# Hi and lo of the MLP activations in one matmul of 512 columns

## The chip, the cores and the metric

The kernel runs on one NeuronCore of a Trainium2 chip. The metric is the device time of one execution in microseconds (us). A run gives a median over several executions; one more execution is profiled, and all rows of a trace come from that one.

## The reference

A four-layer encoder on 256 tokens of width 1024, all in float32. Each layer is a mixer (a state-space layer in layers 0 and 3, dilated attention in 1, differential attention in 2) and an MLP, both with a residual and a norm in front. The change is in the four MLPs:

```python
def rmsnorm(x, g):
    xf = x.astype(jnp.float32)
    y = xf * lax.rsqrt(jnp.mean(xf * xf, axis=-1, keepdims=True) + RMS_EPS)
    return (y * g.astype(jnp.float32)).astype(x.dtype)
...
def sqrelu_mlp(h, w1, w2):
    return jnp.square(jax.nn.relu(h @ w1)) @ w2
...
        x = x + h
        x = x + sqrelu_mlp(rmsnorm(x, norm_mlp_g[i]), mlp_w1[i], mlp_w2[i])
```

`w1` is 1024x4096 and `w2` 4096x1024, so an MLP reads 32 MB of weights for 256 tokens.

## The kernel before

Activations lie transposed: features on the 128 partitions, the 256 tokens (`T`) along the free axis. A product is made of tiles: a 128x128 tile of weights stands in TensorE (a weight load, LDWEIGHTS), and the 256 tokens stream through it (a matmul of 256 columns). Float32 accuracy comes from splitting: every weight and every activation is written as hi + lo in the type fp32r, and a tile product is three matmuls into the same 256 columns of a PSUM bank, hi x hi, hi x lo and lo x hi. That is `mm3`, lines 150, 151 and 152, each matmul with its own weight load. This text calls the work on one weight tile a *trio*.

Weights come in chunks of 128x1024 (512 KB). `_dma` asks SP's queue for a chunk into `raw` (5 buffers), `_conv` makes `whi` on ScalarE (ACT, line 117) and `wlo` on VectorE (DVE, line 119), 5 buffers each; `plan_chunk` fixes the order of the chunks beforehand, `take` and `done` step through it. A chunk feeds 8 trios.

The MLP, `mlp`, runs over 8 strips `s` of 512 hidden features. `up(s)` makes a strip, 4 chunks and 32 trios, into two banks (`r0`/`r1` or `r2`/`r3`), two 256-column results side by side in a bank. `evac(s)` turns it into the input of the second product: on DVE `v` (relu, times the norm's factor, line 358), on ACT the square (line 360) and the hi part `hh` (line 362), on DVE the lo part `hl` (line 363), each on 128x512. `down(s)` multiplies the strip by its rows of `w2`, 4 chunks and 32 trios, and adds to 8 output tiles that lie two to a bank in `a0` to `a3` through the whole MLP. The order is up 0, up 1, down 0, up 2, down 1, and so on; the last strip goes tile by tile (`proj_tail`), and after each tile `finish` adds it to the residual `xT` (line 1179) and makes the next part's split inputs `spl` (lines 234, 235) and squares.

For strip 0, and in the first MLP for strip 4, the first half of the hidden features lies in a tile of its own, `h0`/`l0` (`same` in the code; `h` and `l` in the rows). In the first MLP, after strip 2, `bias_vectors` and `lambdas` use the banks `r2` and `r3` for three small products of the later attention layers (lines 732, 733, 748).

Each engine works through its own queue in order; a scheduler lays out the queues when the kernel is built. The trace's 490 `whi` and 490 `wlo` instructions are all chunks of all parts. Matmuls in plain float32 (line 148, tile `nf`) stand in the two state-space layers.

Of the kernel before, what the change touches and what calls it, by code (L numbers as in the profile page):

```python
# [24 lines left out]
NSPL = 16  # L25
# [26 lines left out]
class Prog:  # L52
# [92 lines left out]
    def mm3(self, out, wh, wl, xh, xl, start, stop):  # L145
# [6 lines left out]
        mm(out, lhsT=wl, rhs=xh, start=False, stop=stop, skip_group_check=True)  # L152

# [65 lines left out]
    def split_tile(self):  # L219
        return self.sp.tile([P, 2, T], F32R, tag="spl", name="spl", bufs=NSPL)  # L220

    def norm_begin(self):
        self.sqs = []
        self.uh, self.ul = [], []

    def norm_split(self, j, g, perm, x):
# [3 lines left out]
        if j % 2 == 0:  # L230
            h, lo = self.split_tile(), self.split_tile()
            self.uh += [h[:, 0, :], h[:, 1, :]]
            self.ul += [lo[:, 0, :], lo[:, 1, :]]
# [60 lines left out]
    def normalised_tiles(self, keep):  # L294
        self.nhl = [self.lp.tile([P, KD, T], F32R, name=n) for n in ("nh", "nl")]
        self.nf = self.lp.tile([P, KD, T], F32, name="nf") if keep else None

    def normalised(self, g_mix):

        nc = self.nc  # L300
        nh, nl = self.nhl
# [5 lines left out]
        return nh, nl  # L307


    def plan_mlp(self, l):  # L310
        w1, w2 = self.a["mlp_w1"], self.a["mlp_w2"]
        def up(s):
            for j in range(4):
                self.plan_chunk(("up", l, s, j), w1[l, j * 256:(j + 1) * 256, s * 512:(s + 1) * 512].rearrange("(k p) f -> p k f", p=P))
        def down(s):
            for j in range(4):
                self.plan_chunk(("dn", l, s, j), w2[l, (4 * s + j) * P:(4 * s + j + 1) * P, :].rearrange("(k p) f -> p k f", p=P))
        up(0)
        for s in range(1, 8):
            up(s)  # L320
            down(s - 1)
        for key, ap in self.tail_chunks(("dn", l), w2[l], 28, 4):
            self.plan_chunk(key, ap)

    def mlp(self, l, finish):
        nc = self.nc
        hs = {}
        acc = [self.bank(f"a{i}") for i in range(4)]

        def up(s):  # L330
            b = [self.bank(f"r{2 * (s % 2) + i}") for i in range(2)]
            for j in range(4):
                wh, wl = self.take(("up", l, s, j))
                for kk in range(2):
                    k = 2 * j + kk
                    for n in range(4):
                        c = slice(kk * 512 + n * P, kk * 512 + (n + 1) * P)
                        self.mm3(b[n // 2][:, (n % 2) * T:(n % 2 + 1) * T], wh[:, c], wl[:, c],
                                 self.uh[k], self.ul[k], k == 0 and n % 2 == 0, k == 7)
# [3 lines left out]

        self.lp.tile([P, 80], F32, name="gap0")
        same = [self.lp.tile([P, 2, T], F32R, name=n) for n in ("h0", "l0")]
        self.lp.tile([P, 48], F32, name="gap1")
        resets = (0,) if self.rep else (0, 4)

        def evac(s, b):
            hh = self.lp.tile([P, 4, T], F32R, tag="hh", name="hh", bufs=2)  # L350
            hl = self.lp.tile([P, 4, T], F32R, tag="hl", name="hl", bufs=2)
            hs[s] = [(hh[:, j, :], hl[:, j, :]) for j in range(4)]
            if s in resets:
                hs[s][:2] = [(same[0][:, j, :], same[1][:, j, :]) for j in range(2)]
            for i in range(2):
                v = self.lp.tile([P, 2, T], F32, tag="v", name="v", bufs=3)
                sq = self.lp.tile([P, 2, T], F32, tag="vsq", name="vsq", bufs=2)
                nc.vector.scalar_tensor_tensor(out=v, in0=b[i].rearrange("p (n t) -> p n t", n=2), scalar=0.0,
                                               in1=self.rbc.unsqueeze(1).to_broadcast([P, 2, T]), op0=ALU.max, op1=ALU.mult)
                nc.scalar.activation(out=sq, in_=v, func=AF.Square)  # L360
                h, lo = (hh[:, 2 * i:2 * i + 2, :], hl[:, 2 * i:2 * i + 2, :]) if i or s not in resets else same
# [3 lines left out]
        def down(s):  # L365
            h = hs.pop(s)
            if s < 7:
                for j in range(4):
                    wh, wl = self.take(("dn", l, s, j))
                    for n in range(8):  # L370
                        c = slice(n * P, (n + 1) * P)
# [794 lines left out]
    def prepare_part(self, i):  # L1166
# [8 lines left out]
        def finish(n, acc, perm=False):  # L1175
# [8 lines left out]
            if nxt == "final":  # L1184
                self.final_tile(n)
# [114 lines left out]
```

## Time and profile before

| what | us |
|---|---|
| runs of the kernel before: median, lowest, highest of 3 | 1605.35, 1604.55, 1608.08 |
| profiled execution: its time | 1607.9 |
| profiled execution: span from the first to the last instruction | 1606.1 |
| TensorE busy in the span | 1566.8 (98%) |
| VectorE busy, ScalarE busy | 1203.5, 960.3 |

The profiled execution's time is 1.8 us over its span and 2.55 us over the median. Busy time of TensorE overlaps itself, since matmuls are pipelined: a row gives each 256-column matmul some 280 ns, while one starts every 113 to 120 ns. What one costs is read from start to start.

### The profile page before, as it was taken

The numbers are of one execution on the slowest core, as the hardware profiler recorded it, in microseconds if no ns is written. First come the engines' busy times: TensorE is split into PE (matmuls) and PEld (weight loads), VectorE is DVE, ScalarE is ACT, GpSimd is POOL, SyncE is SP. The second block draws the span as 40 slices with busy tenths as digits, with TensorE's granted clock in tenths as the row PEclk, the third lists the DMA queues.
The fourth block names the chain that finished last, engine by engine and source line by source line (L and its number), as shares of the span: only waits on it lengthen the run. The fifth ranks groups of instructions, "written<-read, shape, count | busy, mean of one in ns | idle before, by whom it ended". The sixth has DMA issues, their size and how long they took to land.

```text
span 1606.1 us, 32218 instructions
## 1 busy us (share of the span) xinstructions
PE 1566.8 (98%) x12942; PEld 1519.4 (95%) x12942; DVE 1203.5 (75%) x1970; ACT 960.3 (60%) x1620; POOL 134.1 (8%) x120
## 2 busy tenths in 40 slices
PE   9999999999999999999999999999998999999998
PEld 8889899999999999999999999999988988899997
DVE  6999998455697777766556898655588999995554
ACT  6586865444667666655445777444455767664444
POOL 0012121000300000010000101000011122310001
PEclk9999999999999999999999999999999999999999
DMA  7677755676566555546666764666655767656661
GB/s 230 195 223 236 213 188 181 204 223 191 159 200 178 151 170 162 171 148 190 191 196 187 198 193 122 205 192 193 189 163 155 217 210 216 210 173 195 192 193 64
DMA packets 230293, 299.83 MB, mean 187 GB/s; under 512 B 16496, under 2 KB 166256, under 8 KB 230144
## 3 DMA queue, kind: packets, MB, share of 16 engines
q1 hardware_dynamic: 209552, 262.51, 53.4%
q10 hardware_dynamic: 20592, 35.27, 8.0%
q8 instruction: 101, 1.65, 0.4%
q14 instruction: 48, 0.39, 0.1%
HBM read 296.41 MB, written 3.62 MB: 187 GB/s over the span
## 4 chain that ended last, share of the span: by engine, by line
PE 73%; DVE 14%; DMA 5%; ACT 4%; issue 3%; POOL 1%; ACTq 0%; SPq 0%; DVEq 0%; POOLq 0%
PE r L151 12%; PE r L150 12%; PE r L152 12%; PE a L150 8%; PE a L152 8%; PE a L151 8%; DVE wlo L119 3%; DMA raw<-in_ssd_in_w_dram 2%; DMA bc<-scr 2%; PE r L148 2%; DVE cvx L488 1%; PE a L857 1%; PE a L858 1%; PE a L856 1%; DVE bc L582 1%
## 5 line engine op out<-in xcount | busy, mean ns | idle before, releaser
L119 DVE TENSOR_TENSOR wlo<-raw,whi 128x1024 fp32r<-128x1024 f32 (+1 forms) x490 | 592.8, 1217 | 291.4 <-ACT whi L117 287.9
L117 ACT CAST whi<-raw 128x1024 fp32r<-128x1024 f32 (+1 forms) x490 | 503.4, 1034 | 436.3 <-PE r L151 223.6
L151 PE MATMUL r<-spl,whi 128*128 128x256 f32 x1696 | 472.9, 279 | 4.7 <-DVE spl L235 4.7
L150 PE MATMUL r<-spl,whi 128*128 128x256 f32 x1696 | 475.1, 280 | 0.1
L152 PE MATMUL r<-spl,wlo 128*128 128x256 f32 x1696 | 471.4, 278 | 0.4 <-DVE wlo L119 0.4
L151 PEld LDWEIGHTS r<-spl,whi 128*128 128x128 f32 x1696 | 318.4, 188 | 6.5 <-DVE spl L235 6.1
L152 PEld LDWEIGHTS r<-spl,wlo 128*128 128x128 f32 x1696 | 318.6, 188 | 0.7 <-DVE wlo L119 0.6
L150 PEld LDWEIGHTS r<-spl,whi 128*128 128x128 f32 x1696 | 318.2, 188 | 0.6 <-DVE xT L1179 0.3
L150 PE MATMUL a<-hh,whi 128*128 128x256 f32 x944 | 261.4, 277 | 0.0
L151 PE MATMUL a<-hl,whi 128*128 128x256 f32 x944 | 261.3, 277 | 0.0
L152 PE MATMUL a<-hh,wlo 128*128 128x256 f32 x944 | 260.9, 277 | 0.0
L151 PEld LDWEIGHTS a<-hl,whi 128*128 128x128 f32 x944 | 177.6, 188 | 0.0
L150 PEld LDWEIGHTS a<-hh,whi 128*128 128x128 f32 x944 | 177.3, 188 | 0.2 <-ACT whi L117 0.2
L152 PEld LDWEIGHTS a<-hh,wlo 128*128 128x128 f32 x944 | 177.2, 188 | 0.0
L150 PE MATMUL r<-nh,whi 128*128 128x256 f32 x576 | 166.5, 289 | 7.3 <-DVE cvx L488 4.1
L152 PE MATMUL r<-nh,wlo 128*128 128x256 f32 x576 | 163.1, 283 | 1.9 <-DVE wlo L119 1.8
L151 PE MATMUL r<-nl,whi 128*128 128x256 f32 x576 | 162.2, 282 | 0.0
L245 POOL TENSOR_TENSOR sqacc<-sqacc,sq 128x256 f32<-128x256 f32 x48 | 44.5, 927 | 1090.7 <-ACT sq L243 1089.1
L150 PEld LDWEIGHTS r<-nh,whi 128*128 128x128 f32 x576 | 110.4, 192 | 11.8 <-issue 4.2
L152 PEld LDWEIGHTS r<-nh,wlo 128*128 128x128 f32 x576 | 110.1, 191 | 3.2 <-DVE wlo L119 2.3
L151 PEld LDWEIGHTS r<-nl,whi 128*128 128x128 f32 x576 | 109.9, 191 | 0.7 <-issue 0.4
L607 ACT ACTIVATE e<-bc,tb 128x256 f32<-128x256 f32 (+1 forms) x256 | 95.7, 447 | 6.1 <-DVE bc L582 4.8
(246 smaller groups left out, 2521.4 us busy)
## 6 DMA issues: line engine op xcount, KB each, us to landing
raw<-in_mlp_w_dram SPq DMA_DIRECT2D x256, 512.0 KB
raw<-in_ssd_in_w_dram SPq DMA_DIRECT2D x96, 512.0 KB
bc<-scr ACTq DMA_DIRECT2D x32, 768.0 KB
raw<-in_dil_qkv_w_dram SPq DMA_DIRECT2D x48, 512.0 KB
raw<-in_ssd_out_w_dram SPq DMA_DIRECT2D x32, 512.0 KB
raw<-in_dil_qkv_w_dram SPq DMA_DIRECT2D x64, 192.0 KB
raw<-in_diff_qkv_w_dram SPq DMA_DIRECT2D x24, 512.0 KB
raw<-in_dil_out_w_dram SPq DMA_DIRECT2D x8, 512.0 KB
```

The costliest lines, as they stand in the source:

```text
L117: self.nc.scalar.copy(out=hi[:, :n], in_=raw[:, :n])
L119: self.nc.vector.tensor_tensor(out=lo[:, :n], in0=raw[:, :n], in1=hi[:, :n].bitcast(F32), op=ALU.subtract)
L148: mm(out, lhsT=wh, rhs=xh, start=start, stop=stop, skip_group_check=True)
L150: mm(out, lhsT=wh, rhs=xh, start=start, stop=False, skip_group_check=True)
L151: mm(out, lhsT=wh, rhs=xl, start=False, stop=False, skip_group_check=True)
L152: mm(out, lhsT=wl, rhs=xh, start=False, stop=stop, skip_group_check=True)
L245: nc.gpsimd.tensor_tensor(out=self.sqs[0], in0=self.sqs[0], in1=sq, op=ALU.add)
L488: nc.vector.scalar_tensor_tensor(out=u[:, n, lo:hi], in0=b[:, n, lo + d:hi + d], scalar=col("conv_w", w, cc), in1=u[:, n, lo:hi], op0=ALU. ...
L582: nc.vector.tensor_tensor(out=o, in0=o, in1=mask, op=ALU.add)
L607: X = lambda o, i_, bias: nc.scalar.activation(out=o, in_=i_, func=AF.Exp, bias=bias)
L856: mm(o, lhsT=self.uh[k][:, t], rhs=w_h, start=k == 0, stop=False)
L857: mm(o, lhsT=self.uh[k][:, t], rhs=w_l, start=False, stop=False)
```

## The change

In the MLPs, except for the first strip of the first product and the last four weight tiles of the second one's second half, a trio becomes two matmuls: `whi` against hi and lo of the activation at once, 512 columns into a whole bank (hi part's result in columns 0 to 255, lo part's in 256 to 511), and `wlo` against hi, 256 columns into the bank's first half. `mm_wide` is this pair. Split tiles are laid out so that hi and lo can be read as one operand (`halves`). A result of 256 tokens now takes a bank, so a strip of the first product takes four banks (`r0` to `r3` for even strips, `a0` to `a3` for odd ones) and the second product holds only four output tiles at a time: the first product runs over all strips, its hidden features stay in SBUF (`hhl`, 8 buffers), and the second product goes over them twice, once for each half of the output columns. Outside TensorE, `evac` for strips 1 to 7 copies the second half of each bank to SBUF on ACT and adds it to the first on DVE, and `down` adds each tile's second half to the residual. The chunks of `w2` have another shape (two row blocks of 512 columns for one of 1024). In the mixers the matmuls stay as they are; hi and lo of a pair of tiles lie in one tile there too.

```diff
-NSPL = 16
+NSPL = 8
...
+    def mm_wide(self, bank, wh, wl, both, start, stop):
+
+        mm = self.nc.tensor.matmul
+        mm(bank.rearrange("p (a t) -> p a t", a=2), lhsT=wh, rhs=both, start=start, stop=False, skip_group_check=True)
+        mm(bank[:, 0:T], lhsT=wl, rhs=both[:, 0, :], start=False, stop=stop, skip_group_check=True)
...
     def split_tile(self):
-        return self.sp.tile([P, 2, T], F32R, tag="spl", name="spl", bufs=NSPL)
+
+        return self.sp.tile([P, 2, 2, T], F32R, tag="spl", name="spl", bufs=NSPL)
+
+    def halves(self, t, i):
+
+        return t[:, 0, i, :], t[:, 1, i, :], t[:, :, i, :]
...
-        up(0)
-        for s in range(1, 8):
-            up(s)
-            down(s - 1)
-        for key, ap in self.tail_chunks(("dn", l), w2[l], 28, 4):
-            self.plan_chunk(key, ap)
...
+        for hf in range(2):
+            for q in range(16 - 2 * hf):
+                self.plan_chunk(("dn", l, hf, q), w2[l, q * 256:(q + 1) * 256, hf * 512:(hf + 1) * 512].rearrange("(k p) f -> p k f", p=P))
+        for c in range(2):
+            self.plan_chunk(("dn", l, "tail", c), w2[l, 28 * P:32 * P, 512 + c * 256:768 + c * 256].rearrange("(k p) f -> p k f", p=P))
...
         def up(s):
-            b = [self.bank(f"r{2 * (s % 2) + i}") for i in range(2)]
+
+            tags = ("r0", "r1") if s == 0 else [f"{'ra'[s % 2]}{i}" for i in range(4)]
+            b = [self.bank(t) for t in tags]
...
+                        else:
+                            self.mm_wide(b[n], wh[:, c], wl[:, c], self.ub[k][2], k == 0, k == 7)
...
         def evac(s, b):
...
+                if s == 0:
+                    src = b[i].rearrange("p (n t) -> p n t", n=2)
+                else:
+                    src = v
+                    for n in range(2):
+                        nc.scalar.copy(out=sq[:, n, :], in_=b[2 * i + n][:, T:2 * T])
+                        nc.vector.tensor_tensor(out=v[:, n, :], in0=b[2 * i + n][:, 0:T], in1=sq[:, n, :], op=ALU.add)
+                nc.vector.scalar_tensor_tensor(out=v, in0=src, scalar=0.0, in1=self.rbc.unsqueeze(1).to_broadcast([P, 2, T]), op0=ALU.max, op1=ALU.mult)
...
+        def down(hf):
+            acc = [self.bank(f"{'ra'[hf]}{i}") for i in range(4)]
+            for q in range(16 - 2 * hf):
+                wh, wl = self.take(("dn", l, hf, q))
+                for kk in range(2):
+                    for n in range(4):
+                        c = slice(kk * 512 + n * P, kk * 512 + (n + 1) * P)
+                        self.mm_wide(acc[n], wh[:, c], wl[:, c], hs[2 * q + kk][2], q == 0 and kk == 0, q == 15 and kk == 1)
+                self.done()
...
+            for n in range(4):
+                add(4 * hf + n, acc[n][:, T:2 * T])
+                if not hf:
+                    finish(n, acc[n][:, 0:T], final=False)
...
-            down(s - 1)
-        down(7)
+        down(0)
+        down(1)
```

How the queues move at the three places that the prediction speaks of. First TensorE in the second layer's MLP, where the second strip begins; `sqacc` and `sq` are the squares that the norm sums, `r_` and `a_` are banks, `spl` the split input. Before:

```order
L152 MATMUL r_8771<-spl,wlo 128x256
L277 MATMUL a_8886<-sqacc,guard_90 128x256
L277 MATMUL a_8886<-sq,guard_90 128x256
L150 MATMUL r_8915<-spl,whi 128x256
L151 MATMUL r_8915<-spl,whi 128x256
L152 MATMUL r_8915<-spl,wlo 128x256
```

And now, in the same place:

```order
L152 MATMUL r_8346<-spl,wlo 128x256
L290 MATMUL r_8461<-sqacc,guard_90 128x256
L290 MATMUL r_8461<-sq,guard_90 128x256
L157 MATMUL a_8489<-spl,whi 128x512
L158 MATMUL a_8489<-spl,wlo 128x256
L157 MATMUL a_8490<-spl,whi 128x512
L158 MATMUL a_8490<-spl,wlo 128x256
```

Three rows of 256 columns with three weight loads have become two rows, 512 and 256 columns, with two. TensorE's whole queue has 11822 rows before and 9966 now, 1856 fewer.

Second VectorE in the same MLP, in the middle of the strips; `wlo` is the conversion of a chunk, `v` and `hl`/`hhl` belong to `evac`, `rs_y` is the norm's factor. Before, one round (a strip of each product):

```order
L119 TENSOR_TENSOR wlo<-raw,whi 128x1024 x7
L358 SCALAR_TENSOR_TENSOR v<-r_9171,rs_y_8891 128x512
L358 SCALAR_TENSOR_TENSOR v<-r_9172,rs_y_8891 128x512
L119 TENSOR_TENSOR wlo<-raw,whi 128x1024
L363 TENSOR_TENSOR hl<-vsq,hh 128x512 x2
```

And now, one strip of the first product:

```order
L119 TENSOR_TENSOR wlo<-raw,whi 128x1024 x2
L374 TENSOR_TENSOR v<-r_8602,vsq 128x256
L374 TENSOR_TENSOR v<-r_8603,vsq 128x256
L374 TENSOR_TENSOR v<-r_8604,vsq 128x256
L375 SCALAR_TENSOR_TENSOR v<-v,rs_y_8466 128x512
L119 TENSOR_TENSOR wlo<-raw,whi 128x1024
L374 TENSOR_TENSOR v<-r_8605,vsq 128x256
L379 TENSOR_TENSOR hhl<-vsq,hhl 128x512
L375 SCALAR_TENSOR_TENSOR v<-v,rs_y_8466 128x512
L119 TENSOR_TENSOR wlo<-raw,whi 128x1024
L379 TENSOR_TENSOR hhl<-vsq,hhl 128x512
```

A round of 8 conversions with one evacuation has become 4 conversions with one, and the evacuation has four additions more; in the second product VectorE now has conversions alone (14 in a row, then the additions of the half).

Third TensorE in the first layer's MLP, around the small products of `bias_vectors` (`oh`, `tab`) and `lambdas` (`lamt`), which stand in banks `r2` and `r3`. Before they followed a strip that lay in `r0` and `r1`, here as `r_3413` and `r_3414`:

```order
L151 MATMUL r_3414<-spl,whi 128x256
L152 MATMUL r_3414<-spl,wlo 128x256
L732 MATMUL r_3554<-oh,tab 16x512
L733 MATMUL r_3555<-oh,tab 16x128
L150 MATMUL a_3010<-hh,whi 128x256
```

And now they follow strip 2 in `r0` to `r3` (`r_3249` and `r_3250` are `r2` and `r3`), a few rows into strip 3:

```order
L157 MATMUL r_3250<-spl,whi 128x512
L158 MATMUL r_3250<-spl,wlo 128x256
...
L157 MATMUL a_3383<-spl,whi 128x512
L764 MATMUL r_3365<-oh,tab 16x512
L158 MATMUL a_3383<-spl,wlo 128x256
...
L765 MATMUL r_3366<-oh,tab 16x128
L157 MATMUL a_3383<-spl,whi 128x512
L158 MATMUL a_3383<-spl,wlo 128x256
L780 MATMUL r_3376<-lamt,ones 128x2
```

So these three now need banks that the strip just made has to leave first.

## Rows read from the trace of the kernel before

**Rows 1.** The page, engines: busy us, share of the span, instructions.

```profile
PE 1566.8 (98%) x12942; PEld 1519.4 (95%) x12942; DVE 1203.5 (75%) x1970; ACT 960.3 (60%) x1620; POOL 134.1 (8%) x120
```

**Rows 2.** The page, chain that ended last, by engine.

```profile
PE 73%; DVE 14%; DMA 5%; ACT 4%; issue 3%; POOL 1%; ACTq 0%; SPq 0%; DVEq 0%; POOLq 0%
```

**Rows 3.** Windows: us; busy us and instructions begun or running, by engine; PEclk; DMA share, GB/s.

```profile
305.00:360.00 55.00, 55.00 (x469) 55.00 (x468) 28.88 (x28) 24.67 (x28) 0.00 (x0) 1.00 0.71 222
...
724.00:735.00 11.00, 11.00 (x95) 11.00 (x94) 9.78 (x13) 8.17 (x12) 0.00 (x0) 1.00 0.59 173
735.00:872.00 137.00, 137.00 (x1210) 137.00 (x1209) 77.33 (x75) 64.64 (x74) 0.00 (x0) 1.00 0.64 193
1033.00:1160.00 127.00, 127.00 (x1123) 127.00 (x1123) 71.99 (x71) 61.48 (x71) 0.00 (x0) 1.00 0.63 192
1455.00:1570.00 115.00, 115.00 (x1017) 115.00 (x1016) 64.42 (x63) 54.23 (x62) 0.00 (x0) 1.00 0.65 195
```

**Rows 4.** Timeline of TensorE, tile h/l of the first MLP: start us, us, instruction.

```profile
273.84 0.28 PE L150 MATMUL a<-h,whi 128*128 128x256 f32 x1
273.96 0.28 PE L151 MATMUL a<-l,whi 128*128 128x256 f32 x1
274.08 0.28 PE L152 MATMUL a<-h,wlo 128*128 128x256 f32 x1
274.20 0.28 PE L150 MATMUL a<-h,whi 128*128 128x256 f32 x1
274.32 0.28 PE L151 MATMUL a<-l,whi 128*128 128x256 f32 x1
```

**Rows 5.** Timeline of TensorE, 384-column matmuls in layer 1, first and last of 22.

```profile
451.12 0.34 PE L858 MATMUL a<-whi,spl 128*128 128x384 f32 x1
...
454.76 0.34 PE L858 MATMUL a<-whi,spl 128*128 128x384 f32 x1
```

**Rows 6.** Chain in order of time (start us, us, what), plain float32 matmuls of 256 columns.

```profile
70.40 3.45 PE r L148 x16
```

**Rows 7.** Groups of instructions by form, 735 to 872 us: busy us, mean ns | idle before.

```profile
L119 DVE TENSOR_TENSOR wlo<-raw,whi 128x1024 fp32r<-128x1024 f32 x51 | 62.5, 1226 | 57.9 <-ACT whi L117 57.9
L117 ACT CAST whi<-raw 128x1024 fp32r<-128x1024 f32 x50 | 52.7, 1055 | 71.4 <-PE r L151 40.0 <-PE a L151 31.4
L150 PEld LDWEIGHTS a<-hh,whi 128*128 128x128 f32 x207 | 38.9, 188 | 0.0
L358 DVE SCALAR_TENSOR_TENSOR v<-r,rs_y 128x512 f32<-128x512 f32 x12 | 7.8, 687 | 0.0
L363 DVE TENSOR_TENSOR hl<-vsq,hh 128x512 fp32r<-128x512 f32 x12 | 7.8, 688 | 2.0 <-ACT hh L362 2.0
L360 ACT ACTIVATE vsq<-v 128x512 f32<-128x512 f32 x12 | 6.9, 621 | 0.0
L362 ACT CAST hh<-vsq 128x512 fp32r<-128x512 f32 x12 | 6.8, 612 | 0.0
```

**Rows 8.** Groups by form, whole span, 128x256 on DVE and on ACT.

```profile
L1179 DVE TENSOR_TENSOR xT<-xT,a 128x256 f32<-128x256 f32 x38 | 16.1, 438 | 12.3 <-PE a L152 12.3
...
L482 ACT ACTIVATE cvx<-r,vec 128x256 f32<-128x256 f32 x32 | 16.3, 558 | 9.4 <-PE r L148 8.8 <-PE r L152 0.6
L305 ACT CAST nh<-nf 128x256 fp32r<-128x256 f32 x16 | 6.0, 402 | 3.9 <-DVE nf L304 3.9
```

**Rows 9.** Timeline, first MLP, small products and their evacuation.

```profile
294.59 1.03 PE L732 MATMUL r<-oh,tab 32*16 32x512 f32 x2
295.46 0.38 PE L733 MATMUL r<-oh,tab 32*16 32x128 f32 x2
297.62 0.57 ACT L734 COPY bv<-r 16x512 f32<-16x512 f32 x1
298.44 0.67 DVE L735 TENSOR_TENSOR bv<-r,oh 16x512 f32<-16x512 f32 x1
299.18 0.37 PE L748 MATMUL r<-lamt,ones 128*128 128x2 f32 x2
```

More of the change, by code (lines that the diff above doesn't have):

```diff
@@ L143, in split_keys, with mm3 @@
         self.nc.vector.tensor_tensor(out=lo, in0=src, in1=hi.bitcast(F32), op=ALU.subtract)
-    def mm3(self, out, wh, wl, xh, xl, start, stop):
+    def mm3(self, out, wh, wl, xh, xl, both, start, stop):
         mm = self.nc.tensor.matmul
@@ L294, in normalised_tiles @@
     def normalised_tiles(self, keep):
-        self.nhl = [self.lp.tile([P, KD, T], F32R, name=n) for n in ("nh", "nl")]
+        self.nhl = self.lp.tile([P, 2, KD, T], F32R, name="nhl")
         self.nf = self.lp.tile([P, KD, T], F32, name="nf") if keep else None
@@ L300, in normalised @@
         nc = self.nc
-        nh, nl = self.nhl
+        nh, nl = self.nhl[:, 0], self.nhl[:, 1]
         for k in range(KD):
@@ L337, in up @@
                         c = slice(kk * 512 + n * P, kk * 512 + (n + 1) * P)
-                        self.mm3(b[n // 2][:, (n % 2) * T:(n % 2 + 1) * T], wh[:, c], wl[:, c],
-                                 self.uh[k], self.ul[k], k == 0 and n % 2 == 0, k == 7)
+                        if s == 0:
+                            self.mm3(b[n // 2][:, (n % 2) * T:(n % 2 + 1) * T], wh[:, c], wl[:, c], *self.ub[k], k == 0 and n % 2 == 0, k == 7)
+                        else:
+                            self.mm_wide(b[n], wh[:, c], wl[:, c], self.ub[k][2], k == 0, k == 7)
                 self.done()
             return b
[L344 to L347, printed above, removed]
         def evac(s, b):
[L350 to L354, printed above, removed]
+            hhl = self.lp.tile([P, 2, 4, T], F32R, tag="hhl", name="hhl", bufs=8)
+            hs.extend(self.halves(hhl, j) for j in range(4))
+            if s == 0:
+                hs[:2] = [self.halves(same, j) for j in range(2)]
             for i in range(2):
@@ L378, in mlp, with add @@
-        b = up(0)
-        self.norm_rows("a3")
-        evac(0, b)
-        for s in range(1, 8):
+        def add(n, half):
+            nc.vector.tensor_tensor(out=self.xT[:, n, :], in0=self.xT[:, n, :], in1=half, op=ALU.add)
+        def down(hf):
[7 more added lines that the diff above has]
+                self.done()
+                if hf and last and q == 3:
+                    for n in range(4):
+                        self.final_tile(n)
+            for n in range(4):
+                add(4 * hf + n, acc[n][:, T:2 * T])
+                if not hf:
+                    finish(n, acc[n][:, 0:T], final=False)
+            if hf:
+                for m in range(4):
+                    if m % 2 == 0:
+                        wh, wl = self.take(("dn", l, "tail", m // 2))
+                    for i in range(4):
+                        c = slice(i * 256 + (m % 2) * P, i * 256 + (m % 2 + 1) * P)
+                        self.mm3(acc[m][:, 0:T], wh[:, c], wl[:, c], *hs[28 + i], False, i == 3)
+                    finish(4 + m, acc[m][:, 0:T])
+                    if m % 2:
+                        self.done()
@@ L382, in mlp @@
+        for s in range(8):
             b = up(s)
+            if s == 0:
+                self.norm_rows("r3")
             evac(s, b)
@@ L444, in fn @@
                 first = kind == "z" and c0 == 0
-                xh, xl = (self.uh, self.ul) if defer else ([st["n"][0][:, k, :] for k in range(KD)], [st["n"][1][:, k, :] for k in range(KD)])
+                xs = self.ub if defer else st["n"]
                 for i in range(2):
@@ L651, in y @@
             yf = lp.tile([P, 2, T], F32, tag="yf", name="yf", bufs=cfg["n_yf"]) if any(whole) else None
-            yh, yl = (None, None) if all(whole) else (self.split_tile(), self.split_tile())
+            yhl = None if all(whole) else self.split_tile()
             for n in range(2):
@@ L1183, in finish @@
                 self.norm_tile(n, g, nxt == "mix1")
-            if nxt == "final":
+            if nxt == "final" and final:
                 self.final_tile(n)
```

80 lines of the change are left out of this document (33 added, 47 removed).

## The prediction

> **What bounds the kernel now.** I read the page's first part, then the chain, then windows inside the MLPs, then starts of single matmuls. TensorE is busy for 98% of the span, its weight loads for 95%, VectorE for 75% [rows 1]; the chain that ended last lies on TensorE for 73% [rows 2]. Inside the MLPs it is TensorE alone: between 735 and 872 us it has no idle time at all [rows 3]. So an MLP is as long as its stream of matmuls, and what counts is the interval from one start to the next. In the window 1033 to 1160 us 1123 matmuls were begun or running; a matmul's row is 280 ns long, so 2.4 of them ran at the start, and 127 us over 1120.6 gives 113.3 ns. The first MLP's window gives 55 us over 466.6, 117.9 ns [rows 3]. On the tile `h`/`l` four intervals take 0.48 us, 120 ns [rows 4]. The granted clock is 1.00 in all these windows, the 2.4 GHz level, where 256 columns last 106.7 ns. So a matmul pays 6.7 to 13.3 ns beyond its columns, with the same shapes and the same lines; the three levels are a state of the stream that the rows show and don't explain.
>
> **The change on TensorE.** Per MLP 7 strips of 32 trios and 128 + 112 trios of the second product change form: 464, in four MLPs 1856, which is also the number of matmuls and weight loads that disappear. The columns stay: 768 a trio, 320.0 ns. So the whole gain is in what a matmul pays beyond its columns. Now a trio costs 3 x 113.3 = 340.0 ns in the second to fourth MLP.
>
> The trace has no fp32r matmul of 512 columns, so I bound it. The nearest in type is the 384-column one: 21 intervals in 3.64 us, 173.3 ns, 13.3 over its columns [rows 5]. If this surplus belongs to the weight load that runs beside it, 512 columns take 213.3 + 13.3 = 226.6 ns. The nearest in length is the plain float32 matmul: 16 take 3.45 us, 215.6 each [rows 6], which fits two cycles a column (213.3) and 2.3 beyond; its stream is as long as the new one, but takes in half as much per cycle. So the ends are 215.6 and 226.6. I take the middle, 221.1: both rows are equally near, and the 256-column surplus of 6.7 gives almost the same, 220.0. The second matmul, `wlo` with 256 columns, stays as it is, 113.3 (upper end 120 [rows 4]). New trio: 334.4 ns, 5.6 less; 1856 x 5.6 = 10.4 us.
>
> [...]
>
> The first MLP pays 117.9 for a long stretch; at 113.3 its 55 us would be 2.1 shorter. Whether the new stream falls into such a state is open; I count half, 1.0 us.
>
> **VectorE and ScalarE.** Evacuating a strip costs VectorE four additions more, priced by the residual's 128x256 addition from PSUM, 0.44 us [rows 8]. A strip now asks of it 4 conversions of 1.23, 4 additions, two `v` of 0.69 and two lo parts of 0.69 [rows 7]: 4.9 + 1.8 + 2.8 = 9.4 us, against 32 x 334 = 10.7 us of TensorE. ScalarE has 4 conversions of 1.06, four copies between 0.40 and 0.56 (SBUF and PSUM source [rows 8]), two squares of 0.62 and two casts of 0.61 [rows 7]: 8.3 to 8.9. Laid against each other in the order of the queues, where the square waits for `v` and the lo part for the cast, the pair needs about 10 us a strip. So I cost it at nothing, and the cover is twofold: 0.7 us a strip, and the lead of the conversions. ScalarE idles 71.4 us in 50 conversions waiting for TensorE to let a `whi` buffer go [rows 7], so it works as far ahead as five buffers allow, some four chunks or 10 us. Without cover the price is the excess over 10.7 times 28 strips. A strip's banks are wanted again one strip later, and its evacuation ends some 6 us after it.
>
> In the second product VectorE has 1.23 us of work in each chunk of 2.7, so the eight additions a MLP and the first half's residuals lie under the second half; its banks, `a0` to `a3`, have been empty for long. At the end four additions stand ahead of four tiles instead of eight tiles: about even, 0. The weights come in the same bytes, with the DMA engines at 0.64 [rows 3]; 1.6% faster (5.6 of 340) makes that 0.65: nothing.
>
> The small products in the first MLP now need `r2` and `r3` from strip 2. TensorE comes to line 764 about 0.9 us after the strip; by then two copies and three additions have run, the third being that of `r2`. The next needs the fourth addition, behind a conversion, near 3.2 us, when TensorE is there at about 3.3; the last needs the evacuation of the first (0.57 and 0.67 us [rows 9]). Each is within some tenths of its time; I add 0.5 us. Queued behind them are the next strip's matmuls.
>
> **Sum.** -10.4 - 1.0 + 0.5 = -10.9 us. The profiled execution took 1607.9, 2.55 over the median of the runs; it becomes 1597.0 and the median **1594.5 us**.
>
> **The rivals.** *Weight loads are the limit.* They are busy 95% [rows 1], and loads of 188 ns follow every 113 ns [rows 7]. If 113.3 is the time of a load, a trio needs only the columns of the wide matmul, 215.6, and one load, 113.3: 328.9, 11.1 less, 20.6 us, and with the other terms about 1584. Against it: beside 384 columns a load has time to spare, and the matmul still pays 13.3. The Trainium skill (Perfetto Trace Analysis, "Identifying the Most-Contended Engine") judges TensorE's headroom by the busy share of weight loads rather than of matmuls; by that this rival would be the likeliest, and the 384-column rows are why I put it second.
>
> *The surplus doesn't fall.* If the wide matmul pays the upper end and the other 113.3, a trio takes 339.9, as now: 1605.
>
> *The surplus grows with the columns* (the other side). 256 columns pay 6.7 and 384 pay 13.3; carried on, 512 pay 20: 233.3 + 113.3 = 346.6, 6.6 more, +12.3 us, 1617. The stream staying in its 120 ns state gives the same by another way, 226.6 + 120. It decides once the wide matmul exceeds 226.7. For it speaks that longer did pay more; against it, that in the 384-column rows the roles are exchanged (the weights stream, the activation stands), and that plain float32 pays 2.3 over a stream of 512 cycles.
>
> *VectorE becomes the limit of the first product.* If a strip needs 11.4 instead of 10 us, 28 x 0.7 = 20 us of gain are lost and it ends near 1614. It decides at 10.7 us a strip. At the beginning of an MLP VectorE is at 9.78 of 11 us already [rows 3]; the lead makes up for it.
>
> **How the numbers follow.** Forecast 0.40 (1589 to 1600), weight loads 0.20, no fall 0.17, growth 0.14, VectorE 0.09. What a measurement here can tell from no change is 0.2%, 3.2 us. Faster by more: 0.40 + 0.20 and a part of the third, 0.64; within: 0.16; slower: 0.20. The range goes from below the second case to the fifth, 1582 to 1614; it leaves the growth case and a little at either end out. The likeliest case's own range is 1589 to 1600, the times by the two ends of the wide matmul (1584 and 1605) moved inward by a quarter. The mixers' matmuls may change their state when the MLP before them ends otherwise; no row sizes that, and it is in no term.
>
> **What would show it.** Starts in the MLPs: the wide matmul followed after 216 to 227 ns, the narrow one after 113 to 120; windows of the second product without idle TensorE; in the strips ScalarE still waiting for TensorE to free `whi`. The prediction is wrong if the wide matmul takes over 227 ns, if TensorE waits for `wlo` or for a bank inside the strips, or if the narrow matmul, beside which the next wide one's weights are loaded, rises over 120.

## The result and the profile after

The changed kernel takes 1618.97 us (median of 4 runs, 1616.45 to 1620.44) against 1605.61 (1604.55 to 1608.08): 1.0082 of the time before, 95% interval 1.0067 to 1.0096. It is slower, where 1594.5 was forecast. The profiled execution took 1618.64 us with a span of 1616.8; before it was 1607.9 with 1606.1, so the spans differ by 10.7.

The page's engines, and the chain that ended last, by engine and by line (they answer [rows 1] and [rows 2]):

```profile
PE 1582.1 (98%) x11086; PEld 1449.3 (90%) x11086; DVE 1249.5 (77%) x2114; ACT 1008.5 (62%) x1732; POOL 137.8 (9%) x120
...
PE 80%; DVE 10%; ACT 4%; DMA 3%; issue 2%; POOL 0%; SPq 0%; ACTq 0%; DVEq 0%; POOLq 0%
PE a L157 14%; PE r L157 13%; PE r L150 7%; PE a L158 7%; PE r L151 7%; PE r L152 7%; PE r L158 7%; DVE wlo L119 2%; PE a L150 2%; PE a L152 2%; PE a L151 2%; DMA raw<-in_ssd_in_w_dram 2%; PE r L664 1%; PE a L888 1%; PE a L889 1%
```

1856 matmuls and as many weight loads are gone, and the busy share of the loads fell from 95% to 90%, yet TensorE has more of the chain than before (80% against 73%). The windows of [rows 3] once more:

```profile
305.00:360.00 55.00, 55.00 (x313) 47.75 (x312) 39.95 (x54) 35.89 (x52) 0.00 (x0) 1.00 0.66 210
724.00:735.00 11.00, 11.00 (x64) 9.52 (x63) 10.31 (x17) 8.39 (x15) 0.00 (x0) 1.00 0.59 181
735.00:872.00 137.00, 137.00 (x777) 119.00 (x776) 89.52 (x112) 77.73 (x107) 3.39 (x3) 1.00 0.61 186
1033.00:1160.00 127.00, 127.00 (x721) 110.36 (x720) 84.35 (x106) 72.45 (x102) 3.38 (x3) 1.00 0.60 188
1455.00:1570.00 115.00, 115.00 (x653) 99.94 (x652) 75.87 (x97) 67.80 (x97) 3.62 (x3) 1.00 0.60 186
```

TensorE is still never idle inside an MLP, at the 2.4 GHz level (1.00), and VectorE and ScalarE have time to spare: nothing took TensorE's place as the limit. In 127 us there are now 721 matmuls begun or running, 719 without those that ran at the start; two of them make what was a trio, so a pair takes 2 x 127 / 719 = 353 ns. The timeline of TensorE in the second product shows the two intervals (start us, us, instruction):

```profile
819.90 0.40 PE L157 MATMUL r<-hhl,whi 128*128 128x512 f32 x1
820.13 0.28 PE L158 MATMUL r<-hhl,wlo 128*128 128x256 f32 x1
820.25 0.40 PE L157 MATMUL r<-hhl,whi 128*128 128x512 f32 x1
820.49 0.28 PE L158 MATMUL r<-hhl,wlo 128*128 128x256 f32 x1
820.61 0.40 PE L157 MATMUL r<-hhl,whi 128*128 128x512 f32 x1
```

From 819.90 to 820.61 are two pairs. Over all starts of the trace, 472 of 480 wide matmuls here, and 499 of 512 with `spl` into the banks `a`, are followed after 235 ns; the narrow one after 118 or 119. Together 353.3 ns, 848 cycles for 768 columns: 80 cycles beyond the columns, where three matmuls paid 48 (340.0 ns). So one matmul fewer costs 13.3 ns more.

Groups by form, 735 to 872 us (they answer [rows 7]):

```profile
L119 DVE TENSOR_TENSOR wlo<-raw,whi 128x1024 fp32r<-128x1024 f32 x49 | 60.6, 1236 | 46.2 <-ACT whi L117 46.2
L117 ACT CAST whi<-raw 128x1024 fp32r<-128x1024 f32 x49 | 51.6, 1053 | 52.9 <-PE r L157 32.5 <-PE a L157 17.6 <-PE a L158 2.1
L374 DVE TENSOR_TENSOR v<-a,vsq 128x256 f32<-128x256 f32 x12 | 4.7, 423 | 0.0
L373 ACT COPY vsq<-r 128x256 f32<-128x256 f32 x12 | 4.4, 374 | 2.5 <-PE r L158 2.5
```

ScalarE still waits for TensorE to let a `whi` buffer go, 52.9 us in this stretch, so the conversions kept their lead; the new additions take 423 ns and the copies 374.

Where the 10.7 us lie, by sections from one norm's small products (`sqacc`) to the next (starts taken from the traces; TensorE passes through each section in order):

| section, us | MLP 1 | mixer 2 | MLP 2 | mixer 3 | MLP 3 | mixer 4 | MLP 4 |
|---|---|---|---|---|---|---|---|
| before | 176.1 | 282.2 | 171.5 | 119.7 | 170.9 | 248.9 | 167.8 |
| after | 177.6 | 282.2 | 175.8 | 119.7 | 175.8 | 244.3 | 172.6 |

MLPs 2 to 4 lose 4.3, 4.9 and 4.8, the first 1.5, and the last mixer gives 4.6 back. MLP 2 adds up. Of its 512 trios 464 became pairs; the 32 of strip 0 stay, and 16 at the end of the second product (16 weight tiles, not the four named above). Before, the 32 trios of strip 1 ran at 353.3 as well (117.8 a matmul), and the 16 on `h`/`l` at 360. So 416 lose 13.3 ns and 16 gain 6.7, +5.44 us; and a wait at the MLP's end is gone, in the kernel before

```profile
887.44 0.28 PE L150 MATMUL r<-spl,whi 128*128 128x256 f32 x1
888.70 0.39 PE L151 MATMUL r<-spl,whi 128*128 128x256 f32 x1 [0.99 <-DVE spl L235]
```

for the split of the last tiles, 1.26 us from start to start instead of 0.11, since the changed kernel finishes half of the columns earlier: -1.26 with a second interval of 0.22. The sum is +4.2, measured +4.3. The same wait went at the end of MLP 1 (1.3 us) and of MLP 3 (0.6); MLP 4 had none.

The last mixer's 4.6 us are not in the intervals of its 256-column matmuls. Its window (columns as in the windows above), before and after:

```profile
1180.70:1429.60 248.90, 233.57 (x1776) 215.05 (x1775) 227.88 (x367) 161.71 (x315) 50.94 (x28) 0.97 0.63 191
1191.10:1435.40 244.30, 231.66 (x1776) 213.67 (x1775) 227.36 (x366) 162.13 (x315) 51.73 (x28) 0.98 0.64 192
```

TensorE idles 15.3 us in it before and 12.6 after, the mean granted clock is 0.97 and 0.98, and a 256-column matmul with `spl` takes 115.4 ns from start to start in both. In the traces of the experiments this mixer takes between 244.3 and 249.3 us. What sets its length is open.

### The profile page after: what moved, and what is told of

The parts are those of the page before. It is cut to its first block, busy times and chain, and to the rows that moved or that the text cites. A ratio compares the mean times of both kernels' runs of the same rounds, so it can differ in the third digit from the quotient of the medians.

```text
span 1616.8 us, 28753 instructions
## 1 busy us (share of the span) xinstructions
PE 1582.1 (98%) x11086; PEld 1449.3 (90%) x11086; DVE 1249.5 (77%) x2114; ACT 1008.5 (62%) x1732; POOL 137.8 (9%) x120
## 4 chain that ended last, share of the span: by engine, by line
PE 80%; DVE 10%; ACT 4%; DMA 3%; issue 2%; POOL 0%; SPq 0%; ACTq 0%; DVEq 0%; POOLq 0%
PE a L157 14%; PE r L157 13%; PE r L150 7%; PE a L158 7%; PE r L151 7%; PE r L152 7%; PE r L158 7%; DVE wlo L119 2%; PE a L150 2%; PE a L152 2%; PE a L151 2%; DMA raw<-in_ssd_in_w_dram 2%; PE r L664 1%; PE a L888 1%; PE a L889 1%
## 5 line engine op out<-in xcount | busy, mean ns | idle before, releaser
L151 PE MATMUL r<-spl,whi 128*128 128x256 f32 x800 | 223.9, 280 | 2.7 <-DVE spl L248 2.7
L150 PE MATMUL r<-spl,whi 128*128 128x256 f32 x800 | 226.3, 283 | 0.1
L152 PE MATMUL r<-spl,wlo 128*128 128x256 f32 x800 | 223.4, 279 | 1.2 <-DVE wlo L119 1.2
L157 PE MATMUL a<-spl,whi 128*128 128x512 f32 x512 | 182.6, 399 | 0.0
L150 PE MATMUL r<-nhl,whi 128*128 128x256 f32 x576 | 165.8, 288 | 7.3 <-DVE cvx L520 5.0
L157 PE MATMUL r<-hhl,whi 128*128 128x512 f32 x480 | 169.8, 397 | 0.0
L152 PE MATMUL r<-nhl,wlo 128*128 128x256 f32 x576 | 162.6, 282 | 0.6 <-DVE wlo L119 0.6
L151 PE MATMUL r<-nhl,whi 128*128 128x256 f32 x576 | 161.9, 281 | 0.0
L151 PEld LDWEIGHTS r<-spl,whi 128*128 128x128 f32 x800 | 149.5, 187 | 3.7 <-DVE spl L248 3.5
L152 PEld LDWEIGHTS r<-spl,wlo 128*128 128x128 f32 x800 | 150.6, 188 | 1.6 <-DVE wlo L119 1.6
L150 PEld LDWEIGHTS r<-spl,whi 128*128 128x128 f32 x800 | 149.9, 187 | 0.6 <-DVE xT L1209 0.3
L157 PE MATMUL a<-hhl,whi 128*128 128x512 f32 x416 | 147.3, 398 | 0.0
L158 PE MATMUL a<-spl,wlo 128*128 128x256 f32 x512 | 144.0, 281 | 0.0
```

What stands on the lines that cost most here:

```text
L150: mm(out, lhsT=wh, rhs=xh, start=start, stop=False, skip_group_check=True)
L151: mm(out, lhsT=wh, rhs=xl, start=False, stop=False, skip_group_check=True)
L157: mm(bank.rearrange("p (a t) -> p a t", a=2), lhsT=wh, rhs=both, start=start, stop=False, skip_group_check=True)
L158: mm(bank[:, 0:T], lhsT=wl, rhs=both[:, 0, :], start=False, stop=stop, skip_group_check=True)
```

## The experiments

Times of single runs are set beside the kernel before on the same chip. Where the kernel before ran 17 times on one chip, its times lay between 1603.1 and 1609.2 us (e9 to e11) and between 1602.5 and 1609.5 (e12); a difference of 3 us between two single runs shows nothing, so the traces decide there.

**e1, streams by themselves.** 48 rounds each, product into one bank, operands shifted by `d` floats:

```python
...
flow([(0, H, 256, 0), (0, L, 256, 0), (1, H, 256, 0)])   # trio
flow([(0, H, 512, 512), (1, H, 256, 0)])                 # pair, two blocks
flow([(0, H, 512, 512)]); flow([(0, H, 384, 0)]); flow([(0, H, 256, 0)])
...
```

> A kernel with nothing but streams of fp32r matmuls out of SBUF, weights moving on by 128 columns each time, no other engine at work (it computes nothing of the reference). Theory A (a matmul pays by the columns that it streams): 512 columns cost twice 256 whatever the operand's form, 226 to 236 ns, and the pair 512 + 256 as much as three of 256. Theory B (the wide matmul pays for its operand in two blocks): 512 columns in one piece cost 216 to 227, in two blocks 235. Theory C (a fixed price for each weight load): 512 costs 220, 384 166.7 and 128 60 ns if 256 costs 113.3. If the surplus comes from other engines' or the queues' traffic, all of them show 2 to 3 ns over their columns.

Windows inside five streams (columns as in the windows above): trio, pair, 512, 384 and 256 columns alone:

```profile
18.50:34.50 16.00, 16.00 (x135) 16.00 (x135) 0.00 (x0) 0.00 (x0) 0.00 (x0) 1.00 0.00 1
36.00:52.00 16.00, 16.00 (x92) 13.90 (x92) 0.00 (x0) 0.00 (x0) 0.00 (x0) 1.00 0.00 1
104.00:112.00 8.00, 8.00 (x37) 6.64 (x36) 0.00 (x0) 0.00 (x0) 0.00 (x0) 1.00 0.01 2
125.00:133.00 8.00, 8.00 (x48) 8.00 (x47) 0.00 (x0) 0.00 (x0) 0.00 (x0) 1.00 0.01 2
134.00:138.00 4.00, 4.00 (x36) 4.00 (x35) 0.00 (x0) 0.00 (x0) 0.00 (x0) 1.00 0.00 0
```

No other engine works here, and the surplus is there all the same. By the starts: 256 columns in a row 120 ns each, 384 173.3, 512 226.7, so 32 cycles (13.3 ns) beyond the columns whatever their number; the trio 360.0 (96 cycles), which is three of these; but the pair 353.3 (80), not 226.7 + 120 = 346.7. One piece or two blocks, 256 first or 512 first, made no difference. Shifting x by 8 floats against the weights did: trio 350.0, pair 346.7. 128 columns came every 111.7 ns, so a load needs no more than that, and two of them (223 ns) fit into a pair with room. No theory held whole: A had 512 columns right but not the pair, B fell, and C's fixed surplus fits 256, 384 and 512 columns in streams of their own (13.3 ns here), but neither 128 columns nor the pair.

**e2, the wide matmul taken apart,** in the order, banks and evacuation of the changed kernel:

```diff
-        mm(bank.rearrange("p (a t) -> p a t", a=2), lhsT=wh, rhs=both, ...)
+        mm(bank[:, 0:T], lhsT=wh, rhs=both[:, 0, :], ...)
+        mm(bank[:, T:2 * T], lhsT=wh, rhs=both[:, 1, :], ...)
```

> The changed kernel with the wide matmul taken apart into two of 256 columns, into the same two halves of the bank; all else as changed. If the wide instruction is to blame, a trio is back at 340.0 ns in the MLPs, 13.3 less, and the execution some 20 us or more shorter than the changed kernel's, 1595 to 1600. If it is a state of the stream that the new order or layout brings about (theory A), it stays at 353.3 and the time at about 1619.

1608.06 us (before: 1607.28). Two windows of MLP 2, the first in its strips, the second in the second product:

```profile
735.00:790.00 55.00, 55.00 (x469) 55.00 (x468) 43.17 (x60) 38.42 (x59) 0.00 (x0) 1.00 0.62 189
815.00:870.00 55.00, 55.00 (x486) 55.00 (x485) 29.67 (x32) 24.26 (x29) 2.44 (x3) 1.00 0.61 192
```

The changed kernel has 313 in each of these. The 469 of the strips is 117.8 ns a matmul, the 486 of the second product 113.3. So taking the wide instruction apart gives back about 11 us, half of what was expected, because a trio has two levels here. Order, banks and evacuation of the change cost nothing in the total that this run can tell from the kernel before; MLPs 2 to 4, at 173.1, 173.1 and 170.9, are 1.6 to 3.1 us longer than there, by the strips at 117.8.

**e3, hi and lo of x next to each other,** so that the wide matmul reads one piece:

```diff
-        return t[:, 0, i, :], t[:, 1, i, :], t[:, :, i, :]
+        return t[:, i, 0, :], t[:, i, 1, :], t[:, i, :, :]
...
```

> The changed kernel with hi and lo of a tile next to each other, so that the wide matmul reads 512 columns in one piece (the evacuations then write in two pieces). Theory B (two blocks cost): the wide matmul falls from 235 to 216 to 227 ns, some 15 to 30 us shorter than the changed kernel. Theory A (by columns): it stays near 235 or moves together with the narrow one (118.3) to another level of the same ratio.

1621.71, the wide matmul still 235 and the narrow one 118. The two blocks are not the cause.

**e4, offsets and history.** Streams of 24 rounds into four banks in turn, x shifted by `d` against the weights, some behind 16 rounds at another offset, some in groups:

```python
for r in (8, 16, 24, 32, 40, 48, 56):
    flow(trio(r), 16); flow(trio(0)); flow(trio(r), 16); flow(pair(0))
for d in range(4, 64, 4): flow(trio(d))
for d in range(4, 64, 4): flow(pair(d))
for d in (0, 8, 16):
    for g in (2, 4, 8): flow(pair(d), group=g)
...
```

> Computes nothing of the reference: streams of matmuls on TensorE alone, 24 rounds each, with the product going to four banks in turn, as in the MLPs. Theory A (the surplus is set by a state of the stream, that is by where the moving operand lies against the weights and by what ran just before): the trio of 256 columns, 360.0 ns at offset 0 in the first study, falls to 340 (113.3 a matmul) after 16 rounds with the operand moved by some offset of 8 to 56 floats, or at some constant offset; the pair 512 + 256, 353.3 ns at offset 0, stays between 346 and 353 everywhere, since two unlike lengths in turn lose the good state. Theory B (the pair's surplus is a property of the 512-column instruction alone): then 512 columns in a row, 226.7 each at offset 0, and pairs sent in groups (two, four or eight wide matmuls, then as many narrow ones) also cost about 353 a pair; by theory A groups of four or eight cost near 226.7 + 120 = 346.7 at offset 0, and less at the offset where the trio is at its fastest. Theory C (a fixed price for each weight load, 32 cycles at 2.4 GHz or 13.3 ns): every pair at 346.7, in turn or in groups, which the first study already speaks against (353.3).

Windows: the trio at 48 floats behind one stream and behind another, the pair at 48 and at 8, and 512 columns alone at 8:

```profile
178.60:183.60 5.00, 5.00 (x44) 5.00 (x44) 0.00 (x0) 0.00 (x0) 0.00 (x0) 1.00 0.00 0
192.90:197.90 5.00, 5.00 (x46) 5.00 (x45) 0.00 (x0) 0.00 (x0) 0.00 (x0) 1.00 0.00 0
...
455.00:462.40 7.40, 7.40 (x45) 6.43 (x44) 0.00 (x0) 0.00 (x0) 0.00 (x0) 1.00 0.00 0
371.00:378.00 7.00, 7.00 (x43) 6.20 (x42) 0.00 (x0) 0.00 (x0) 0.00 (x0) 1.00 0.00 0
...
568.90:574.00 5.10, 5.10 (x23) 4.12 (x22) 0.00 (x0) 0.00 (x0) 0.00 (x0) 1.00 0.00 0
```

The first two are one stream, instruction for instruction; by the starts its trio took 353.3 ns the first time and 340.0 the second. It is the offset of the MLPs: in the built kernels `whi` and `wlo` begin on multiples of 256 bytes, `spl` and `hhl` (before: `spl`, `hh`, `hl`) 192 bytes, 48 floats, past one, and the small tile `hl0` (before: `h0`, `l0`) on one. Over the 16 offsets the trio took 340.0 to 360.0, the pair in turn 346.5 to 353.7, at 48 floats 353.3 as in the kernel, and at one offset (0) 346.5 to 346.8 or 353.2 to 353.7 by what ran before. Groups gave 342.6 to 350.8, 512 columns alone 226.9 to 233.4. So neither number belongs to an instruction; and no pair in turn came down to the trio's best.

**e5, the kernel before with h0 and l0 at the offset of the rest.**

```diff
-        self.lp.tile([P, 80], F32, name="gap0")
+        self.lp.tile([P, 128], F32, name="gap0")
         same = [self.lp.tile([P, 2, T], F32R, name=n) for n in ("h0", "l0")]
-        self.lp.tile([P, 48], F32, name="gap1")
```

> The kernel before, with one size changed: the two tiles h0 and l0, which two weight tiles of the second product read in strips 0 and 4, are moved by 48 floats, so that they lie against the weights as every other moving tile of the MLPs does (192 bytes past a multiple of 256) and no longer on a multiple of 256. Theory A (the 340.0 ns of a trio is a state, which those 48 matmuls at another offset put the stream into): without them the trios of the MLPs stay at the 353.3 ns (117.8 a matmul) that the stream has behind the mixers, so MLPs 2 to 4 get 13.3 ns x about 490 trios = 6.5 us longer each, and the time is 1620 to 1632. Theory B (the length of a matmul depends on its own operands alone): no change, 1605 to 1608.

1627.21 (before: 1605.52). The windows of e2 hold

```profile
735.00:790.00 55.00, 55.00 (x469) 55.00 (x469) 30.89 (x31) 26.30 (x32) 0.00 (x0) 1.00 0.62 190
815.00:870.00 55.00, 55.00 (x469) 55.00 (x468) 29.79 (x29) 23.97 (x28) 0.00 (x0) 1.00 0.60 190
```

where the kernel before has

```profile
735.00:790.00 55.00, 55.00 (x487) 55.00 (x486) 30.12 (x29) 25.06 (x28) 0.00 (x0) 1.00 0.64 191
815.00:870.00 55.00, 55.00 (x488) 55.00 (x487) 32.08 (x33) 27.20 (x33) 0.00 (x0) 1.00 0.64 194
```

The same matmuls in the same order are 21.7 us apart by the place of two small tiles, 18.4 of them inside the four MLPs by the traces (2.3, 5.4, 5.4 and 5.3): 340.0 ns a trio is a level that the 48 matmuls of `h0` and `l0` switch on, and that stays. This fixes what the changed kernel had to beat: beside a stream at 353.3, as here, its 1618.97 us would have been the shorter time.

**e6, hhl moved by 8 floats** (gap1 from 48 to 56).

> The changed kernel with hhl moved by 8 floats (32 bytes) against the weights; spl stays. Theory A (address and history set the surplus): the pairs of the second product, 353.3 ns at 48 floats in the kernel and in the stream study, go to the 346.7 of the study at 56 floats, the pairs of the first product stay at 353.3; 896 x 6.7 ns = -6 us, 1613. In no case does a pair fall under 346. Theory B (the 512-column matmul has its own price of 235): no change, 1619 to 1622.

1619.73, no change: a miss of the size. The timeline of the second product shows that the intervals did move,

```profile
820.54 0.39 PE L157 MATMUL r<-hhl,whi 128*128 128x512 f32 x1
820.77 0.28 PE L158 MATMUL r<-hhl,wlo 128*128 128x256 f32 x1
820.89 0.40 PE L157 MATMUL r<-hhl,whi 128*128 128x512 f32 x1
821.13 0.28 PE L158 MATMUL r<-hhl,wlo 128*128 128x256 f32 x1
821.25 0.39 PE L157 MATMUL r<-hhl,whi 128*128 128x512 f32 x1
```

from 235 each time to 229 and 240 in turn, with the same sum: the pairs of `hhl` took 353.4 ns, where the study had 346.7 at this offset. The time is the one that theory B gave, though the intervals were not constant as it has it. The level of a stream could not be read off its offset.

**e7, e2 with the switching matmuls in strip 0:** k-tiles 4 and 5 of x are copied to `hl0` and read there.

> The version that takes the wide matmul apart again into two of 256 columns (1608.1), with one addition: in strip 0 the k-tiles 4 and 5 of x are read from the tile hl0, into which ScalarE has copied them, and which lies on a multiple of 256 bytes, as in the kernel before only tiles of h did. Theory A: these 48 matmuls put the stream into the state of 113.3 a matmul before strip 1, so the 896 trios of the first product in strips 1 to 7 go from 353.3 to 340.0, as many as ran at 117.8: up to -11.9 us, 1596 to 1600, below the kernel before. Theory B: no change, 1608.

1611.83, a miss, but the timeline of MLP 2 tells why (us between starts of one line: 0.36 is 120 ns a matmul, 0.34 is 113):

```profile
714.65 0.28 PE L150 MATMUL r<-hl,whi 128*128 128x256 f32 x1
...
715.01 0.28 PE L150 MATMUL r<-hl,whi 128*128 128x256 f32 x1
...
716.07 0.28 PE L150 MATMUL r<-spl,whi 128*128 128x256 f32 x1
...
716.41 0.28 PE L150 MATMUL r<-spl,whi 128*128 128x256 f32 x1
...
718.11 0.59 PE L291 MATMUL r<-sqacc,guard 128*128 128x256 f32 x2
718.54 0.59 PE L291 MATMUL r<-sq,guard 128*128 128x256 f32 x2
...
719.33 0.28 PE L157 MATMUL a<-spl,whi 128*128 128x256 f32 x1
...
719.68 0.28 PE L157 MATMUL a<-spl,whi 128*128 128x256 f32 x1
```

Behind `hl` the stream does run at 113.3; then the norm's two float32 products come (two rows each in the trace), and behind them it is at 117.8, 0.35 between starts of one line. The copies also cost: in the first and the last MLP the first rows of strip 1 now stand ahead of those of `hl`, and TensorE waits there for a `wlo` (2.96 us idle). Two k-tiles of a strip are 8 weight tiles, so the switching matmuls are 24 an MLP, not the 48 that the expectations of e7, e9 and e12 name.

**e8, the changed kernel with four wide matmuls, then four narrow ones.**

```diff
-                    for n in range(4):
+                    for part, n in [(i, n) for i in range(2) for n in range(4)]:
...
```

> The changed kernel with the matmuls of a k-tile in another order: the four wide ones of a row of weight tiles, then the four narrow ones; the same 1856 pairs. Theory A: lengths that change less often lose less: the study had 342.6 to 350.8 a pair in groups of four or eight against 353.3 in turn, so -4 to -15 us, 1604 to 1615. Theory B (the 512-column matmul costs 235 wherever it stands): no change, 1619 to 1622.

1607.32 (before: 1605.52), 11.7 less than the changed kernel, with the same 1856 pairs; MLPs 2 to 4 take 173.3, 173.3 and 170.1. The windows of e2 hold 320 and 318 matmuls, 347 ns a pair;

```profile
735.00:790.00 55.00, 55.00 (x320) 48.05 (x319) 42.91 (x60) 38.56 (x61) 0.00 (x0) 1.00 0.63 192
815.00:870.00 55.00, 55.00 (x318) 47.97 (x317) 29.54 (x32) 23.59 (x28) 2.70 (x3) 1.00 0.62 191
```

a narrow matmul is mostly at 113.3 again, a wide one between 225 and 236.

**e9, the switching matmuls behind the norm's products:** e2 with k-tiles 0 and 1 read from `hl0` in strip 1, and the first k-tiles of h beside the others.

```diff
+            if s == 0:
+                for i in range(2):
+                    nc.scalar.copy(out=x1[i][2], in_=self.ub[i][2].bitcast(F32))
...
-                            self.mm_wide(b[n], wh[:, c], wl[:, c], self.ub[k][2], k == 0, k == 7)
+                            self.mm_wide(b[n], wh[:, c], wl[:, c], (x1 if s == 1 and k < 2 else self.ub)[k][2], k == 0, k == 7)
```

> The version that takes the wide matmul apart into two of 256 columns (1608.1), with the 48 matmuls at a multiple of 256 bytes put behind the norm's small products: k-tiles 0 and 1 of x are read from hl0 in strip 1 (ScalarE copies them there while strip 0 runs), and the first two k-tiles of h lie beside the others. In the run before (e7) the same 48 matmuls in strip 0 did set 113.3 ns a matmul, and the f32 products of the norm that follow ended it at 117.8. Theory A (state): strips 1 to 7 of the first product run at 340.0 a trio, 224 trios x 13.3 ns = -3.0 us per MLP, about -12 in all: 1594 to 1599, 0.992 to 0.996 of the kernel before. Theory B (the address alone): 1608, as e2.

1606.31 (12 runs) against 1606.56 (17 runs), 0.9999 [0.9989, 1.0008]: the total is a miss, MLPs 2 to 4 are not: 170.3, 170.3 and 167.7 us, as expected 3 less than in e2. The first MLP takes 177.0, 4.1 more than in e2. Windows of it ahead of and behind the small products at 285 to 289 us, in e9:

```profile
275.00:283.00 8.00, 8.00 (x73) 8.00 (x72) 6.57 (x9) 5.63 (x9) 0.00 (x0) 1.00 0.68 197
300.00:355.00 55.00, 55.00 (x469) 55.00 (x468) 42.60 (x56) 38.49 (x58) 0.00 (x0) 1.00 0.69 220
```

and in e2:

```profile
275.00:283.00 8.00, 8.00 (x71) 8.00 (x70) 5.52 (x8) 5.26 (x7) 0.00 (x0) 1.00 0.66 198
300.00:355.00 55.00, 55.00 (x486) 55.00 (x485) 42.77 (x56) 39.21 (x58) 0.00 (x0) 1.00 0.68 223
```

e9 goes into them at 113.3 and comes out at 117.8; e2 goes in at 117.8 and comes out at 113.3.

**e10, the changed kernel with the same 8 weight tiles of strip 1 in trios at the other offset.**

> The changed kernel with the same 16 weight tiles of strip 1, and these alone, taken apart into three matmuls of 256 columns that read x at a multiple of 256 bytes; all other pairs as they were. Theory A in its strong form (a pair has a good state too, 346.7 in the stream study, and history picks it): up to 1840 x 6.7 ns = -12 us, 1607 to 1611. Weak form (in the kernel the pair at 48 floats stays at 353.3 whatever came before, as behind the trio-formed strip 0): 1618 to 1621. No theory gives less than 1606, since no pair in turn was under 346.6 in the study.

The expectation's 16 weight tiles are a miscount: the trace has 32 matmuls more than the changed kernel's, 8 an MLP. 1621.01, the weak form: all 512 wide matmuls of `hhl` into the banks `r` stay at 235. What switches a stream of 256 columns does nothing for the pairs at this offset.

**e11, e8 in groups of eight.**

> The changed kernel with the eight wide matmuls of a whole chunk first, then its eight narrow ones (groups of four: 1607.3, 347 a pair). If changes of length are what is lost, and nothing else, half as many changes give back another 1 to 6 us: 1601 to 1606 (the study's best for groups of eight was 342.6 a pair, its others 348.8 and 350.0). If the address and the history decide among the streams of one length (226.7 or 233 a wide matmul, 113.3 to 120 a narrow one), no gain: 1606 to 1612.

1611.17. The MLPs are those of e8 (172.9, 172.9, 170.2); what the total has more lies in the last mixer, 247.9 instead of 244.3, in which nothing was changed. Fewer changes of length bring no more.

**e12, e9 with the first MLP of e2.**

> Three matmuls of 256 columns again, with the 48 matmuls at a multiple of 256 bytes in strip 1 for MLPs 2 to 4 (as e9) and, for the first MLP alone, at the first two k-tiles of h (as e2). In e9 strip 1 of the first MLP ran at 113.3 a matmul until the small products in strip 3 (the ones that read oh and lamt), and the stream came out of them at 117.8 and stayed there; in e2 it went in at 117.8 and came out at 113.3. Theory A (history sets the state, at both places): the first MLP as in e2 (172.9 us from norm to norm), the others as in e9 (170.3, 170.3, 167.7): 4.1 us less than e9, about 1602, 0.9965 to 0.9985 of the kernel before, and so below both kernels. Theory B (the first MLP is slower for a reason of its own, not the state): 1606, no change to the kernel before.

1602.25 (12 runs) against 1606.23 (17 runs), 0.9974 [0.9963, 0.9985]: below both kernels, with the MLPs at 173.3, 170.3, 170.3 and 167.7. It has the weight order and the evacuation of the change and the three matmuls of the kernel before.

## Why the prediction was wrong

**What bounds the kernel: right.** TensorE has no idle time in the MLPs after either, and the starts of its matmuls account for what the MLPs lose.

**The failed step is the price of the wide matmul,** in "The trace has no fp32r matmul of 512 columns, so I bound it": 215.6 to 226.6, taken 221.1, with the narrow one left at 113.3. Measured in its place: 235.0 + 118.3 = 353.3 ns, not 334.4, and 13.3 more than before instead of 5.6 less. Two things were wrong in it. The upper end, 32 cycles beyond the columns as in [rows 5], is the price of 512 columns in a stream of their own at offset 0 (226.7, e1), but at other offsets such a stream took up to 233.4, and a pair in turn need not be the sum of two such prices (353.3 against 226.7 + 120, e1). The lower end came from rows of plain float32, of which the trace has two for each matmul of the queue; no fp32r stream here came near its 2.3 ns beyond the columns. And the 113.3 was carried over as if it belonged to 256 columns with a load beside them, although the prediction itself called it a state of the stream: e5 shows that it was switched on by two tiles, and e10 that the pairs at this offset are not reached by that switch. The change took a stream at its best level, 48 cycles for 768 columns, and put in its place a form whose best in any stream taken in turn was 64 and which in this kernel runs at 80.

**The mechanism by which the surplus grows is not settled.** It hangs on the address of the moving operand against the weights, on what ran before and on the order of lengths; it needs no other engine, and it is neither a price per load (the pair has one less and pays more) nor the two blocks of the operand (e3). What makes these levels, no run here shows.

**The rivals.** *Surplus grows, or the stream stays in its 120 ns state* had the right sign and, with 1617, nearly the right time: the point from which it "decides", 226.7, was passed. But its pair of 346.6 was 6.7 short. The time fitted by luck: many trios had been at 353.3 before, waits at the ends of three MLPs went, and the last mixer gave 4.6 back. *Weight loads are the limit* falls as the price of the new form: a pair has two loads, 128 columns bound each at 111.7 ns (e1), and it took 353.3. Whether loads bound the trio at its best, 113.3 ns against these 111.7, is open: no run separates them. The Trainium skill (Perfetto Trace Analysis, "Identifying the Most-Contended Engine") reads TensorE's headroom from the busy share of loads, beside MFU; here that share fell by 5 points where the same work took 0.8% longer, so it did not show this limit. *VectorE becomes the limit* falls by the idle times of ScalarE, still waiting for TensorE, and by e12, whose strips in MLPs 2 to 4 have the same evacuation and run at 113.3 a matmul.

**The other terms.** Evacuation at nothing: right (423 and 374 ns a piece, against 0.44 and 0.40 to 0.56). The trio's 340.0 was taken for all 464 trios of MLPs 2 to 4; 48 of them in each ran at 353.3 or 360. The first MLP: -1.0 forecast, it lost 1.5 and not the 4.3 to 4.9 of the others, since about half of its trios were at 353.3 before as well. The 0.5 for the small products can't be told apart. The waits at the ends of MLPs 1 to 3 that went (1.3, 1.3 and 0.6 us) were not forecast; nor the last mixer's 4.6, which the prediction left out as a possible change of state in the mixers' matmuls: the intervals there are the same, and idle time and granted clock differ.

## What to carry to other kernels

Before pricing a matmul that the trace does not hold, ask at which level the stream around it runs, and price the whole repeating group (here a pair against a trio), not its members; a short stream of that group by itself, at the kernel's addresses, is a sign of it and no more: it gave the kernel's 353.3 at 48 floats (e4) and missed it at 56 (346.7 against 353.4, e6). If a kernel's rows show two prices for the same instruction, any change of order, length or address may change the price for all that follows, and by more than the change is worth: here 21.7 us by the place of two tiles. Look for the small products between streams: in e2, e7 and e9 the level changed there.

## What the runs showed of the hardware

All at the 2.4 GHz level, with fp32r operands and a new weight load for each matmul:

- Streams of 256-column matmuls ran at 113.3, 117.8 and 120 ns in the MLPs, 16, 26.7 and 32 cycles beyond the columns; in e4 trios at other offsets also lay between these. At one address a stream can have two of them (353.3 and 340.0 a trio, e4), and it kept one for some 1360 matmuls (e9: 113.3 from 726 to 880 us).
- Behind a norm's two float32 products it ran at 117.8, ahead of them at 113.3 (e7); behind other small products one stream went from 113.3 to 117.8 (e9) and another from 117.8 to 113.3 (e2), within a strip.
- 512 and 256 columns in turn cost 346.5 to 353.7 ns, more than three times 256 at their best (340.0) and less than at their worst (360.0). The Trainium skill (TensorE: Matmul & The Clock Gate, "Back-to-back issue gap") gives N / 2.4 + 2.5 ns for an isolated matmul and says that for long ones in a stream with weight loads this counts too much. By that formula an estimate for the pair is 325 ns and for 512 columns 215.8; here the pair took 353.3 in the kernel and 512 columns alone 226.7 (e1), more and not less, so the measurement decides.
